# Turning the stored sums of a Strassen-type down-projection: block transposes and transfers through memory in place of TensorE transposes

## The chip, the cores and the metric

One Trainium2 chip; the kernel runs on one core. The metric is the device time of one execution in microseconds (us). Engines in the profile: PE is TensorE (PEld its weight loads), DVE VectorE, ACT ScalarE, POOL GpSimd, SP SyncE.

## The reference, cut to what matters

One layer of a trunk: attention and a short gated convolution side by side, merged by gates, then a squared-ReLU MLP, then a gated per-layer embedding. Sequence 256, width 2048, MLP width 8192, all float32. The change lies in the MLP:

```python
h = rms_norm(r, g_mlp[i])
r = r + jnp.square(jax.nn.relu(h @ w_up[i])) @ w_down[i]
h = rms_norm(r, g_ple[i])
r = r + jax.nn.sigmoid(h @ w_ple_gate[i]) * (p[i] @ w_ple_proj[i])
```

## The kernel before, in words

Float32 matmuls are done in two parts: each operand is split into a high and a low part (`high` on ScalarE, `low` on VectorE), and three products of the parts are added in PSUM.

The MLP is one loop, `for g in range(NU)`, of 72 steps of a little over 8 us each. In step g TensorE runs `cols(...)`, a unit of the up-projection (64 units, tile `ps_up`) or, in the last 8 steps, of a part of the down-projection that is done plainly (`ps_dn`). From step 7 these sums have only one of the eight PSUM banks, bank 7. Beside it in the step `products` runs the rest of the down-projection by seven products P1 to P7 of sums of quarters of the operands (the scheme of Strassen and Winograd), each in a bank of its own. The weights for that are made by VectorE and ScalarE one step ahead (`make`: `b`, `t13`, `t24`, `s`, `s_raw`), and ScalarE copies the unit's sum out of bank 7 within `make` (`take`, `evacuated`: tiles `up`, `dn`). `load` issues weight transfers on SP's queue; the accumulating transfers go on GpSimd's queue, among them `t<-raw_s` (line 704), which adds one weight block to another on its way.

The seven products belong to two halves of the output rows ("sides"). At the end of a group they are stored to memory, `part_...` (`store`), and added up there. For the stored groups, `fetch_part(side, h)` brings the parts back at steps 53, 56, 59 and 62 into four tiles `part_in`, VectorE adds them with scales in ten jobs, three a step (`run_jobs`), and each call ends in two sums of [256 tokens × 256 columns], u = 4·side + h and 4·side + 2 + h, which lie tokens first. The residual `r_kept[u]` in memory lies columns first, so each sum must be turned.

Before, `turn_part` does it on TensorE: four transposes of 128 × 128 into `ps_part`, in bank 7, between two runs of `products`; `out` copies the bank on ScalarE into a tile `part_out`, and GpSimd issues a transfer that adds it to `r_kept[u]` (line 883). `turns_due`, `queue` and `due` fix that one sum is turned in a step. `load_r` (line 958) reads `r_kept` back: u = 4 to 7 at step 64, 0 and 1 at step 68, 2 and 3 at step 69.

All small tiles come from one pool with one tag (`slot`) and rotate: a tile gets the room of the tile that was handed out a full round earlier, and its first writer waits until all that read that one are done, transfers included. GpSimd's queue issues in the order of the code; each of its transfers takes one of 8 semaphores in turn, and so also waits for the transfer 8 places before it.

Of the kernel before, what the change touches and what calls it, by code (L numbers as in the profile page):

```python
# [18 lines left out]
P = 128  # L19
# [19 lines left out]
def hybrid_block_kernel(ctx: ExitStack, tc: tile.TileContext, ins: dict, out: bass.AP):  # L39
# [29 lines left out]
    def bank(name):  # L69
        return psum("acc", [P, CW], name)  # L70
# [665 lines left out]
    def make(a, xs, evacuate, work):  # L736


        w, j = wS[a], a[1]
        raw = w["raw"]  # L740
        flat, halves = "p a f -> p (a f)", "p (a f) -> p a f"
        fresh = None
        if 0 in xs:
            if j not in sums:
                fresh = sum_u(j)
                sums[j] = tuple(slot([P, 4, P], F32R, f"s_{i}") for i in range(2))
            sh, sl = sums[j]
            for i, name in enumerate(("S1", "S3", "S2", "S4")):
                w[name] = sh[:, i, :], sl[:, i, :]
            if a in NATIVE:  # L750
                w["S1"], w["S3"] = fresh[:, 0, :], fresh[:, 1, :]
                fresh, sh, sl = (t[:, 2:, :] for t in (fresh, sh, sl))
            hi, lo = half_tiles("b")
            keep(w, ("B11", "B22"), hi, lo)
            src = raw[:, 0:2, :].rearrange(flat)
            high(hi, src)
            evacuate()
            if fresh is not None:
                high(sh, fresh)
            low(lo, src, hi)  # L760
            if a in ADDED:
                t13 = w["t13"]
            else:
                t13 = raw[:, 0:3:2, :]
                dve.tensor_add(t13, raw[:, 0:2, :], raw[:, 2:3, :].to_broadcast([P, 2, CW]))
            w["raw13"] = t13
        if 2 in xs:
            b21 = w["B21"] = tuple(slot([P, CW], F32R, f"b21_{n}") for n in range(2))
            high(b21[0], raw[:, 3, :])
            evacuate()  # L770
            out_turned()
            fill()
            dve.tensor_add(raw[:, 1, :], raw[:, 1, :], w["raw13"][:, 0, :])
            if 0 in xs:
                low(b21[1], raw[:, 3, :], b21[0])
                dve.tensor_add(raw[:, 3, :], raw[:, 1, :], raw[:, 3, :])
                raw24 = raw[:, 1:4:2, :]
            else:
                dve.tensor_add(raw[:, 2, :], raw[:, 1, :], raw[:, 3, :])
                low(b21[1], raw[:, 3, :], b21[0])  # L780
                raw24 = raw[:, 1:3, :]
                work()
        if 0 in xs:
            if fresh is not None:
                low(sl, fresh, sh)
            if 2 not in xs:
                work()
            out_turned()
            if a in NATIVE:
                w["T1"], w["T3"] = w["raw13"][:, 0, :], w["raw13"][:, 1, :]  # L790
                fill()
            else:
                t13 = half_tiles("t13")
                keep(w, ("T1", "T3"), *t13)
                view = [t.rearrange(halves, a=2) for t in t13]
                high(view[0], w["raw13"])
                fill()
                low(view[1], w["raw13"], view[0])
        if 2 in xs:
            t24 = half_tiles("t24")  # L800
            keep(w, ("T2", "T4"), *t24)
            view = [t.rearrange(halves, a=2) for t in t24]
            high(view[0], raw24)
            fill()
            low(view[1], raw24, view[0])
# [37 lines left out]
    def scaled(dst, src, by, other, how=ALU.add):  # L843
        dve.scalar_tensor_tensor(dst, src, by, other, op0=ALU.mult, op1=how)

    jobs, turns_due = [], []

    def fetch_part(side, h):
        tiles = {}
        for names in (("P2", "P4"), ("P3", "P5"), ("P1", "z"), ("P7", "P6")):  # L850
            t = slot([P, 2, S], F32, "part_in")
            for i, name in enumerate(names):
                tiles[name] = t[:, i, :]
                if name != "z":
                    load(tiles[name], parts[side, name][:, h * S:(h + 1) * S])
        p1, p2, p3, p4, p5, p6, p7, z = (tiles[n] for n in ("P1", "P2", "P3", "P4", "P5", "P6", "P7", "z"))

        def first():
            act(z, p1, AF.Copy, scale=up0)
            act(p1, p1, AF.Copy, scale=up1)  # L860

        jobs.extend((
            first,
            lambda: scaled(p7, p7, up1, p1),
            lambda: scaled(p2, p2, up0, z),
            lambda: scaled(p7, p6, up1, p7),
            lambda: scaled(z, p5, up0, z, ALU.subtract),
            lambda: scaled(p4, p4, up1, p7),
            lambda: (scaled(p3, p3, up0, z), turns_due.append((4 * side + h, (p2, p4)))),
            lambda: scaled(p5, p5, up1, p7, ALU.subtract),  # L870
            lambda: (scaled(p3, p6, down0, p3), turns_due.append((4 * side + 2 + h, (p3, p5)))),
        ))

    def turn_part(u, src):
        ps = bank("ps_part").rearrange("p (i s) -> p i s", i=2)
        for i in range(2):
            for t in range(NT):
                inorder(nc.tensor.transpose(ps[:, i, t * P:(t + 1) * P], src[t][:, i * P:(i + 1) * P], ident))

        def out():  # L880
            st = slot([P, 2, S], F32, "part_out")
            act(st, ps, AF.Copy)
            nc.gpsimd.dma_start(r_kept[u], st, accum_op=ALU.add)

        turned_out.append(out)

    filling, turned_out = [], []

    def out_turned():
        while turned_out:  # L890
            turned_out.pop(0)()

    def fill(n=1):
        for _ in range(min(n, len(filling))):
# [62 lines left out]
        r[u] = slot([P, 2, S], F32, f"r_{u}")  # L957
        nc.gpsimd.dma_start(r[u], r_kept[u])

    fetching = {53: (1, 0), 56: (1, 1), 59: (0, 0), 62: (0, 1)}  # L960

    for g in range(2):
        load_raw(g)
# [6 lines left out]
    for g in range(NU):  # L970
# [10 lines left out]
        for a, x in staged[g + 2]:  # L981
            if x == 0:
                load_added(a)
        if g in fetching:
            fetch_part(*fetching[g])
        for u in {NU - 8: (4, 5, 6, 7), NU - 4: (0, 1), NU - 3: (2, 3)}.get(g, ()):
            load_r(u)
        if g == NU - 3:
# [39 lines left out]
            dn_done(*units[n][1], evac.pop(n))  # L1028
        taken = []

        queue = [] if ending else list(staged[g - 1])

        def take():
            if taken:
                return
            taken.append(evacuated(ps, kind))
            if ending:
                side = staged[g - 1][0][0][0]
                filling.extend(lambda name=name: store(side, name) for name in NAMES)
            if due and queue:  # L1040
                products(*queue.pop(0))
                turn_part(*due.pop(0))

        due = [turns_due.pop(0)] if turns_due and queue else []

        def run_jobs():
            for _ in range(min(3, len(jobs))):
                jobs.pop(0)()

        fill(carried)  # L1050
        if staged[g]:
            make(staged[g][0][0], [x for _, x in staged[g]], take, run_jobs)
        take()
        out_turned()
        if g == NU - 1:
            p1 = [evacuated(prod["P1"], "p1", by) for by in (up0, up1)]
            d, e = (slot([P, CW], F32, n) for n in "de")
# [12 lines left out]
        if kind == "up" and i == 63:  # L1070
            up_sum(i, evac.pop(g))
            up_high(i)
            up_low(i)
        for a, x in queue:
            products(a, x)
        assert not due
    assert not jobs and not turns_due

# [183 lines left out]
```

## Time and the profile before

| what | number |
|---|---|
| median of 3 runs | 1423.03 us (1422.92 to 1423.10) |
| the profiled execution | 1422.78 us, span 1421.0 us |
| TensorE clock granted | full in all slices |
| `ps_part` transposes | 32, from 1196.1 to 1285.8 us |
| `r_kept<-part_out` issues | 8, from 1197.6 to 1290.0 us |
| `r<-r_kept` issues | 8, from 1237.9 to 1302.1 us |

The span is the time from the first to the last instruction of the profiled execution, and all times of the trace are counted from its start. A row of a timeline reads: start, length, engine, line, operation, tile written <- tiles read, and in brackets the idle time of that engine just before it and what ended it.

### The profile page before, as it was taken

Reading aid. Unit: us, or ns where it says so; the run is one execution under the profiler, and the core shown is the slowest. Engines: PE = TensorE matmul, PEld = TensorE weight load, DVE = VectorE, ACT = ScalarE, POOL = GpSimd, SP = SyncE. Lnnn points to the kernel's source line nnn. Section 1 sums busy time; section 2 is a strip of 40 time slices with the busy share of each in tenths; the row PEclk is TensorE's granted clock in tenths of the full one; section 3 lists DMA queues with packets and bytes.
Section 4 is the critical chain, followed back from the end, with each engine's and each line's share of the span. In section 5 each row is a group of like instructions: output and inputs, shape, how many; then the busy total and the mean of one; then the engine's idle time right before and its main releaser. Section 6 shows DMA issues by size and latency. Waiting matters only on the chain.

```text
span 1421.0 us, 19899 instructions
## 1 busy us (share of the span) xinstructions
PE 1410.7 (99%) x7031; PEld 1192.5 (84%) x7031; DVE 1103.0 (78%) x1685; ACT 880.8 (62%) x1441; POOL 209.6 (15%) x319
## 2 busy tenths in 40 slices
PE   9999999999999999999999999999999999999998
PEld 7888888888888888888888888888888888778888
DVE  7666666766455656665999999999999997798984
ACT  7665544554535444446777777777777876666752
POOL 0034464311120200000010101101010100121000
PEclk9999999999999999999999999999999999999999
DMA  9868787765666675663788887989899899999470
GB/s 295 298 216 262 220 243 229 235 224 198 217 202 213 214 259 194 218 210 107 214 291 239 271 243 236 271 256 271 254 239 276 230 297 279 295 266 275 151 257 23
DMA packets 222708, 333.50 MB, mean 235 GB/s; under 512 B 13840, under 2 KB 147216, under 8 KB 208528
## 3 DMA queue, kind: packets, MB, share of 16 engines
q1 hardware_dynamic: 202944, 287.08, 61.9%
q0 software_dynamic: 19520, 45.11, 14.0%
q8 instruction: 55, 0.90, 0.2%
q14 instruction: 45, 0.37, 0.1%
q10 hardware_dynamic: 144, 0.04, 0.0%
HBM read 294.43 MB, written 24.64 MB: 225 GB/s over the span
## 4 chain that ended last, share of the span: by engine, by line
PE 95%; DMA 2%; DVE 1%; issue 1%; ACT 1%; POOL 0%; SPq 0%; DVEq 0%; POOLq 0%; ACTq 0%
PE ps_up L90 24%; PE P L90 18%; PE ps_g L90 12%; PE ps_o L90 7%; PE ps_pg L90 6%; PE ps_y L90 6%; PE ps_q L90 3%; PE ps_k L90 3%; PE ps_cx L90 3%; PE ps_cb L90 3%; PE ps_cc L90 3%; PE ps_v L90 3%; PE ps_dn L90 1%; PE ps_proj L90 1%; DMA t<-raw_s 1%
## 5 line engine op out<-in xcount | busy, mean ns | idle before, releaser
L101 DVE TENSOR_TENSOR w_lo<-raw,w_hi 128x512 fp32r<-128x512 f32 (+1 forms) x524 | 468.0, 926 | 187.1 <-ACT w_hi L87 161.5
L87 ACT ACTIVATE w_hi<-raw 128x512 fp32r<-128x512 f32 (+1 forms) x524 | 406.9, 816 | 258.9 <-PE ps_g L90 62.6
L90 PE MATMUL ps_up<-x,w_hi 128*128 128x512 f32 x1024 | 255.0, 392 | 0.0
L90 PEld LDWEIGHTS ps_up<-x,w_hi 128*128 128x128 f32 x1024 | 192.1, 188 | 39.3 <-issue 1.7
L90 PE MATMUL ps_g<-w_hi,x 128*128 128x512 f32 x512 | 158.1, 389 | 0.0
L87 ACT ACTIVATE t_hi<-raw_s 128x1024 fp32r<-128x1024 f32 x88 | 93.4, 1062 | 85.3 <-DVE raw_s L101 85.0
L90 PEld LDWEIGHTS ps_up<-x,w_lo 128*128 128x128 f32 x1024 | 131.3, 191 | 5.0
L90 PE MATMUL ps_up<-x,w_lo 128*128 128x256 f32 x1024 | 132.8, 283 | 0.0
L90 PE MATMUL P<-t_hi,s 128*128 128x512 f32 x316 | 115.3, 391 | 0.0
L90 PEld LDWEIGHTS ps_g<-w_hi,x 128*128 128x128 f32 x512 | 96.1, 188 | 19.9
L101 DVE TENSOR_TENSOR t_lo<-raw_s,t_hi 128x1024 fp32r<-128x1024 f32 x88 | 106.3, 1220 | 5.6 <-ACT t_hi L87 5.5
L101 DVE TENSOR_TENSOR raw_s<-raw_s 128x512 f32<-128x512 f32 (+1 forms) x120 | 100.1, 834 | 4.1
L90 PE MATMUL ps_g<-w_lo,x 128*128 128x512 f32 x256 | 99.6, 389 | 0.0
L704 POOL DMA_DIRECT2D t<-raw_s x24 | 20.5, 854 | 454.8 <-DMA raw_s<-in_w_down_dram 121.4
L90 PE MATMUL ps_y<-w_hi,x 128*128 128x512 f32 x256 | 79.4, 389 | 0.0
L87 ACT ACTIVATE up<-ps_up 128x512 f32<-128x512 f32 x64 | 37.9, 593 | 57.7 <-PE ps_up L90 54.0
L101 DVE TENSOR_TENSOR b_lo<-raw_s,b_hi 128x1024 fp32r<-128x1024 f32 x56 | 68.2, 1218 | 4.0 <-ACT b_hi L87 3.9
L90 PEld LDWEIGHTS P<-t_hi,s 128*128 128x128 f32 x316 | 59.4, 188 | 12.0
L90 PE MATMUL ps_pg<-x,w_hi 128*128 128x512 f32 (+1 forms) x272 | 67.9, 380 | 0.7 <-DVE x L101 0.7
L90 PE MATMUL P<-t_lo,s 128*128 128x512 f32 x158 | 61.5, 389 | 0.0
L87 ACT ACTIVATE a<-a 128x256 f32<-128x256 f32 x128 | 53.2, 415 | 12.5 <-DVE a L101 10.6
L87 ACT ACTIVATE b_hi<-raw_s 128x1024 fp32r<-128x1024 f32 x56 | 58.8, 1050 | 0.1
(240 smaller groups left out, 2569.5 us busy)
## 6 DMA issues: line engine op xcount, KB each, us to landing
raw<-in_w_up_dram SPq DMA_DIRECT2D x64, 1024.0 KB, 7.5
raw<-in_w_in_dram SPq DMA_DIRECT2D x56, 1024.0 KB, 5.4
raw_s<-in_w_down_dram SPq DMA_DIRECT2D x200, 256.0 KB, 4.5
raw<-in_w_branch_dram SPq DMA_DIRECT2D x16, 1024.0 KB, 5.8
raw<-in_w_o_dram SPq DMA_DIRECT2D x16, 1024.0 KB, 5.0
raw_first<-in_w_qkv_dram SPq DMA_DIRECT2D x48, 256.0 KB, 6.4
raw<-in_w_qkv_dram SPq DMA_DIRECT2D x12, 1024.0 KB, 6.5
t<-in_w_down_dram SPq DMA_DIRECT2D x48, 256.0 KB, 5.4
```

The source lines that it names most:

```text
L87: return inorder(nc.scalar.activation(*args, **kw))
L90: return inorder(nc.tensor.matmul(*args, **kw))
L101: return lambda *args, **kw: inorder(getattr(nc.vector, name)(*args, **kw))
L704: nc.gpsimd.dma_start(wS[a]["t13"], raw[:, 0:2, :], accum_op=ALU.add)
```

## The change

`fetch_part` becomes `add_parts`. The jobs are eleven and run four a step. The last additions of each sum are followed by a job `turn`: VectorE transposes the sum in blocks of 32 × 32 into a pair of `part_in` tiles that are no longer needed (P1 and z for the first, P7 and P6 for the second). One step later `out` writes this to memory (`turned_s`, two transfers of 128 KB), another step later `back` reads it with `turn_in` (four transfers of 64 KB, in pieces of 32 floats) into a new `part_out`, so that the blocks come to their turned places, and one step after that the accumulating transfer into `r_kept[u]` is issued. What is due stands in `later`, by step, and is issued at the start of the step, before `add_parts` and `load_r`. All these transfers are on GpSimd's queue. The pairs of parts are loaded in another order. `turn_part`, its `out`, `out_turned`, `turns_due`, `queue` and `due` are gone: 32 transposes on TensorE, 8 copies on ScalarE and the use of bank 7 for them. New are 8 block transposes, 16 transfers out and 32 back.

```diff
+        for names in (("P1", "z"), ("P7", "P6"), ("P2", "P4"), ("P3", "P5")):
+            t = pairs[names[0]] = slot([P, 2, S], F32, "part_in")
...
+        def turn(u, src, room):
+            flat = "p a s -> p (a s)"
+            dve.transpose(room.rearrange(flat), src.rearrange(flat))
+            rows_out = turned_room(f"turned_s_{u}", columns=S)
+
+            def out():
+                for t in range(NT):
+                    nc.gpsimd.dma_start(rows_out[t * P:(t + 1) * P, :], room[:, t, :])
+
+            def back():
+                st = slot([P, 2, S], F32, "part_out")
+                turn_in(st, rows_out)
+                later.setdefault(step[0] + 1, []).append(lambda: nc.gpsimd.dma_start(r_kept[u], st, accum_op=ALU.add))
+
+            later.setdefault(step[0] + 1, []).append(out)
+            later.setdefault(step[0] + 2, []).append(back)
...
-            lambda: (scaled(p3, p3, up0, z), turns_due.append((4 * side + h, (p2, p4)))),
+            lambda: scaled(p3, p3, up0, z),
+            lambda: turn(4 * side + h, pairs["P2"], pairs["P1"]),
+            lambda: scaled(p3, p6, down0, p3),
             lambda: scaled(p5, p5, up1, p7, ALU.subtract),
-            lambda: (scaled(p3, p6, down0, p3), turns_due.append((4 * side + 2 + h, (p3, p5)))),
+            lambda: turn(4 * side + 2 + h, pairs["P3"], pairs["P7"]),
...
-    def turn_part(u, src):
-        ps = bank("ps_part").rearrange("p (i s) -> p i s", i=2)
-        for i in range(2):
-            for t in range(NT):
-                inorder(nc.tensor.transpose(ps[:, i, t * P:(t + 1) * P], src[t][:, i * P:(i + 1) * P], ident))
-
-        def out():
-            st = slot([P, 2, S], F32, "part_out")
-            act(st, ps, AF.Copy)
-            nc.gpsimd.dma_start(r_kept[u], st, accum_op=ALU.add)
...
+        step[0] = g
+        for work in later.pop(g, ()):
+            work()
+        if g in adding:
+            add_parts(*adding[g])
...
-            if due and queue:
-                products(*queue.pop(0))
-                turn_part(*due.pop(0))
...
-            for _ in range(min(3, len(jobs))):
+            for _ in range(min(4, len(jobs))):
                 jobs.pop(0)()
```

`turn_in` is an older function of the kernel, used for the attention's and the convolution's tiles:

```python
    def turn_in(dst, src):
        blocks = src.rearrange("(a i) (n b j) -> b i n a j", i=32, b=4, j=32)
        for b in range(4):
            nc.gpsimd.dma_start(dst[b * 32:(b + 1) * 32].rearrange("i n (a j) -> i n a j", j=32), blocks[b])
```

On GpSimd's queue, around the accumulate into `r_kept` of u = 7, there stood before (`t13` is the tile that the trace calls `t`; what is in brackets are the semaphores waited for):

```order
L704 DMA t13_11358<-raw_s_11457 128x1024 [waits DMAHW1_49,DMAHW2_49,DMASW5_49,DMAHW3_49,DMASW1_49,DMAHW4_49,DVE_49,PE_49]
L883 DMA r_kept_5_4719<-part_out_11613 128x512 [waits DMASW6_49,Activation_49]
L704 DMA t13_11535<-raw_s_11624 128x1024 [waits DMAHW0_49,DMAHW2_49,DMASW7_49,DMAHW3_49,DMASW2_49,DMAHW7_49,DVE_49,PE_49]
L883 DMA r_kept_7_4721<-part_out_11704 128x512 [waits Activation_49]
L958 DMA r_4_11819<-r_kept_4_4718 128x512 [waits DMASW3_49,PE_49]
```

and now:

```order
L704 DMA t13_11365<-raw_s_11464 128x1024 [waits DMAHW2_49,DMAHW3_49,DMAHW1_49,DMAHW4_49,DMASW3_49,PE_49]
L420 DMA part_out_11551<-turned_s_5_11451 32x16x32 [waits DMASW1_49,DMASW0_49]
L420 DMA part_out_11551<-turned_s_5_11451 32x16x32 x3
L867 DMA turned_s_7_11530<-part_in_11110 128x256 [waits DVE_49]
L867 DMA turned_s_7_11530<-part_in_11110 128x256
L872 DMA r_kept_5_4719<-part_out_11551 128x512 [waits DMASW6_49,DMASW5_49,DMASW7_49,DMASW4_49,DMASW2_49]
L420 DMA part_out_11641<-turned_s_7_11530 32x16x32 [waits DMASW1_49,DMASW0_49,DMASW3_49,DVE_49,Activation_49]
L420 DMA part_out_11641<-turned_s_7_11530 32x16x32
L704 DMA t13_11548<-raw_s_11636 128x1024 [waits DMAHW3_49,DMAHW2_49,DMAHW7_49,DMAHW0_49,PE_49]
L420 DMA part_out_11641<-turned_s_7_11530 32x16x32 x2
L872 DMA r_kept_7_4721<-part_out_11641 128x512 [waits DMASW6_49,DMASW7_49,DMASW4_49,DMASW3_49]
```

Between the accumulates of u = 5 and u = 7 there are now four transfers back, two of them behind the accumulate of `t`, and the transfers out of u = 7 stand ahead of the accumulate of u = 5.

On TensorE, at the end of step 62, there stood before:

```order
L90 MATMUL P3_10775<-b_hi_11593,s_0_11591 128x512
L90 MATMUL P3_10775<-b_lo_11594,s_0_11591 128x512
L90 MATMUL P3_10775<-b_hi_11593,s_1_11592 128x512
L878 MATMUL ps_part_11699<-ident_90,part_in_11110 128x128 x4
L90 MATMUL P5_10779<-t13_11358,s_raw_11586 128x512
L90 MATMUL P7_10783<-t13_11358,s_raw_11586 128x512
L90 MATMUL ps_up_63_11724<-x_4789,w_hi_11675 128x512
```

and now:

```order
L90 MATMUL P3_10775<-b_hi_11613,s_0_11611 128x512
L90 MATMUL P3_10775<-b_lo_11614,s_0_11611 128x512
L90 MATMUL P3_10775<-b_hi_11613,s_1_11612 128x512
L90 MATMUL P5_10779<-t13_11365,s_raw_11606 128x512
L90 MATMUL P7_10783<-t13_11365,s_raw_11606 128x512
L90 MATMUL ps_up_63_11739<-x_4789,w_hi_11693 128x512
```

The four transposes are gone from between the products; the rest of the order is the same. By step, the block transposes stand in 56 (u = 4), 57 (6), 59 (5), 60 (7), 62 (0), 63 (2) and 65 (1 and 3), and the accumulates are issued in 59, 60, 62, 63, 65, 66 and 68 (both).

More of the change, by code (lines that the diff above doesn't have):

```diff
@@ L770, in make @@
             evacuate()
-            out_turned()
             fill()
@@ L787, in make @@
                 work()
-            out_turned()
             if a in NATIVE:
@@ L844, in scaled, with add_parts @@
         dve.scalar_tensor_tensor(dst, src, by, other, op0=ALU.mult, op1=how)
[L846 to L851, printed above, removed]
+    jobs, later = [], {}
+    def add_parts(side, h):
+        tiles, pairs = {}, {}
+        for names in (("P1", "z"), ("P7", "P6"), ("P2", "P4"), ("P3", "P5")):
+            t = pairs[names[0]] = slot([P, 2, S], F32, "part_in")
             for i, name in enumerate(names):
@@ L868, in fetch_part @@
             lambda: scaled(p4, p4, up1, p7),
-            lambda: (scaled(p3, p3, up0, z), turns_due.append((4 * side + h, (p2, p4)))),
+            lambda: scaled(p3, p3, up0, z),
+            lambda: turn(4 * side + h, pairs["P2"], pairs["P1"]),
+            lambda: scaled(p3, p6, down0, p3),
             lambda: scaled(p5, p5, up1, p7, ALU.subtract),
-            lambda: (scaled(p3, p6, down0, p3), turns_due.append((4 * side + 2 + h, (p3, p5)))),
+            lambda: turn(4 * side + 2 + h, pairs["P3"], pairs["P7"]),
         ))
-    def turn_part(u, src):
-        ps = bank("ps_part").rearrange("p (i s) -> p i s", i=2)
-        for i in range(2):
-            for t in range(NT):
-                inorder(nc.tensor.transpose(ps[:, i, t * P:(t + 1) * P], src[t][:, i * P:(i + 1) * P], ident))
-        def out():
-            st = slot([P, 2, S], F32, "part_out")
-            act(st, ps, AF.Copy)
[L883 to L891, printed above, removed]
+    filling, step = [], [0]
     def fill(n=1):
@@ L958, in load_r @@
         nc.gpsimd.dma_start(r[u], r_kept[u])
-    fetching = {53: (1, 0), 56: (1, 1), 59: (0, 0), 62: (0, 1)}
+    adding = {53: (1, 0), 56: (1, 1), 59: (0, 0), 62: (0, 1)}
     for g in range(2):
@@ L983, in hybrid_block_kernel @@
                 load_added(a)
-        if g in fetching:
-            fetch_part(*fetching[g])
+        step[0] = g
[3 more added lines that the diff above has]
+            add_parts(*adding[g])
         for u in {NU - 8: (4, 5, 6, 7), NU - 4: (0, 1), NU - 3: (2, 3)}.get(g, ()):
@@ L1029, in hybrid_block_kernel @@
         taken = []
-        queue = [] if ending else list(staged[g - 1])
         def take():
@@ L1039, in take @@
                 filling.extend(lambda name=name: store(side, name) for name in NAMES)
-            if due and queue:
-                products(*queue.pop(0))
-                turn_part(*due.pop(0))
-        due = [turns_due.pop(0)] if turns_due and queue else []
         def run_jobs():
-            for _ in range(min(3, len(jobs))):
+            for _ in range(min(4, len(jobs))):
                 jobs.pop(0)()
@@ L1053, in hybrid_block_kernel @@
         take()
-        out_turned()
         if g == NU - 1:
@@ L1073, in hybrid_block_kernel @@
             up_low(i)
[L1074 to L1077, printed above, removed]
+        if not ending:
+            for a, x in staged[g - 1]:
+                products(a, x)
+    assert not jobs and not later
     half_of = {(n, h): (NU + n // 2 + (1 - h) * LEAD // 2, n % 2) for n in range(LEAD) for h in range(2)}
```

## The prediction

> **What bounds the kernel now.** I read the page first: its busy times and its chain that ended last.
>
> ```profile
> span 1421.0 us, 19899 instructions
> PE 1410.7 (99%) x7031; PEld 1192.5 (84%) x7031; DVE 1103.0 (78%) x1685; ACT 880.8 (62%) x1441; POOL 209.6 (15%) x319
> PE 95%; DMA 2%; DVE 1%; issue 1%; ACT 1%; POOL 0%; SPq 0%; DVEq 0%; POOLq 0%; ACTq 0%
> ```
>
> TensorE is the bound: busy 99% of the span and 95% of the chain. Work taken off it counts, as long as nothing else then arrives late. Next, the instructions on the tile that goes, and TensorE's waits from 1150 to 1320 us, the part of the run in which the stored sums are turned.
>
> ```profile
> L878 PE MATMUL ps_part<-ident,part_in x32: 270/273/329, 1196.1 to 1285.8; 128*128 128x128 f32 x32
> L87 ACT ACTIVATE part_out<-ps_part x8: 579/597/601, 1196.7 to 1286.1; 128x512 f32<-128x512 f32 x8
> ...
> PE ps_part L878 <- ACT dn L87: 1.8, 2, 1.5
> ...
> PE ps_dn L90 <- ACT part_out L87: 0.6, 1, 0.6
> PE ps_part L878 <- ACT up L87: 0.6, 1, 0.6
> ```
>
> So 32 transposes stand in 90 us of a run of 1421, and TensorE waits three times for bank 7 on their account, since they, the step's own sum and the next step's sum all use that one bank: 1.8 + 0.6 + 0.6 = 3.0 us. The timeline of TensorE shows what one turn of four costs, and the starts of some steps:
>
> ```profile
> 1241.20 3.70 PE L90 MATMUL ps_dn<-x,w_hi 128*128 128x512 f32 x15
> ...
> 1250.74 0.66 PE L878 MATMUL ps_part<-ident,part_in 128*128 128x128 f32 x4 [1.49 <-ACT dn L87]
> 1251.15 0.48 PE L90 MATMUL P<-t_hi,s 128*128 128x512 f32 x1
> ...
> 1252.40 3.57 PE L90 MATMUL ps_dn<-x,w_hi 128*128 128x512 f32 x15
> ...
> 1287.09 3.56 PE L90 MATMUL ps_dn<-x,w_hi 128*128 128x512 f32 x15
> ```
>
> Matmuls overlap, so the price is from one start to the next: 1251.15 − 1250.74 = 0.41 us for four, not 4 × 0.273. Step 64 lasts from 1241.20 to 1252.40 = 11.2 us; the four steps from 1252.40 to 1287.09 take 8.7 on average. Step 64 is where this stretch is weakest.
>
> The windows of the trace say how full the other resources are (columns: length, busy time of PE, PEld, DVE, ACT, POOL, then granted clock, DMA share, GB/s):
>
> ```profile
> 1050.00:1100.00 50.00, 50.00 (x259) 42.95 (x259) 46.85 (x62) 36.65 (x55) 5.26 (x7) 1.00 1.00 266
> ...
> 1198.00:1215.00 17.00, 17.00 (x89) 13.73 (x87) 15.79 (x28) 12.99 (x21) 2.19 (x3) 1.00 1.00 296
> ...
> 1233.00:1252.00 19.00, 17.18 (x89) 13.77 (x88) 15.90 (x26) 12.20 (x20) 2.79 (x5) 1.00 0.77 251
> 1252.00:1270.00 18.00, 17.36 (x94) 14.59 (x93) 17.25 (x28) 11.98 (x17) 3.44 (x4) 1.00 1.06 279
> 1270.00:1287.00 17.00, 16.66 (x93) 14.14 (x92) 12.49 (x21) 9.69 (x13) 3.95 (x5) 1.00 1.02 291
> ...
> 1303.00:1320.00 17.00, 15.28 (x81) 12.22 (x80) 14.86 (x26) 9.48 (x16) 0.00 (x0) 1.00 0.49 167
> ```
>
> The DMA engines are full almost throughout, and the change gives work to them. That they are full is not in itself a loss: from 1050 to 1100 the share is 1.00 and TensorE is busy 50.00 of 50.00 us. What counts is which transfer is waited for.
>
> **The change part by part.**
>
> *Transposes removed.* 8 turns × 0.41 = 3.3 us off TensorE, all of it on the path.
>
> *Waits on bank 7 removed.* 3.0 us as above. The largest, 1.49 us at 1250.74, comes from a late copy of the step's sum; without the transposes the next user of the bank is the following step's first matmul, several products later, so I take the wait as gone. Gain so far: 3.3 + 3.0 = 6.3 us.
>
> *ScalarE's copies removed.* 8 × 0.597 = 4.8 us, on an engine busy 12.20 of 19.00 us at its busiest there: no direct gain.
>
> *Block transposes added to VectorE.* The same operation stands earlier in this kernel, on the same 128 × 512 floats (from the rows of its tile), and transfers out and back of the new kind have rows too (GpSimd's busy time and mean ns of one issue; then KB and median us to landing):
>
> ```profile
> L101 DVE STREAM_TRANSPOSE blocks<-q x4: 665/685/705, 75.5 to 105.6; 128x512 f32<-128x512 f32 x4
> ...
> L420 POOL DMA_DIRECT2D uT<-turned_uT x16 | 10.7, 704 | 5.9 <-issue 3.9 <-DMA qkT<-turned_q 1.8
> ...
> turned_uT<-blocks POOLq DMA_DIRECT2D x4, 256.0 KB, 3.0
> uT<-turned_uT POOLq DMA_DIRECT2D x16, 64.0 KB, 6.2
> turned_cbT<-blocks POOLq DMA_DIRECT2D x4, 256.0 KB, 4.5
> cbT<-turned_cbT POOLq DMA_DIRECT2D x16, 64.0 KB, 3.7
> ```
>
> 8 × 0.685 = 5.5 us. Two of them fall in step 65, where VectorE has 18.00 − 17.25 = 0.75 us free: 2 × 0.685 − 0.75 = 0.6 us late. Elsewhere 17 − 15.79 = 1.2 us (step 59 and 60) or more covers one. Cost 0.6 us (0 if the next step takes it up, 1.4 if not covered at all).
>
> *Four jobs a step in place of three, and the parts loaded in another order.* The same additions run in the same window; I cost them at nothing, with VectorE's free time above as the cover.
>
> *Transfers added.* Each sum is written out (2 × 128 KB), read back (4 × 64 KB) and then accumulated as before: 8 × 512 KB = 4.2 MB. The page has the two kinds of queue:
>
> ```profile
> q1 hardware_dynamic: 202944, 287.08, 61.9%
> q0 software_dynamic: 19520, 45.11, 14.0%
> ```
>
> q0 moved 45.11 MB in 14.0% of 1421 us, 227 GB/s of all engines; q1 326 GB/s. So the new work is 4.2/326 = 12.9 to 4.2/227 = 18.5 us of all 16 engines. The hole in the windows is 0.23 × 19 = 4.4 us, in 1233 to 1252, and 0.51 × 17 = 8.7 us after 1303. The engines therefore run some 8 to 14 us behind until about 1303, and then catch up. Most of what is behind is loaded a step or more ahead. What is not is in these rows: ScalarE's waits from 1165 to 1320 us, GpSimd's timeline, one row of the chain, the timelines of ScalarE and VectorE, and the landings of `part_out`.
>
> ```profile
> ACT t_hi L87 <- DMA t<-raw_s: 5.2, 2, 3.9
> ...
> ACT x L87 <- DMA r_kept<-part_out: 1.4, 1, 1.4
> ...
> 1227.93 0.85 POOL L704 DMA_DIRECT2D t<-raw_s  x1 [3.51 <-DMA part_in<-part_P]
> 1232.74 0.85 POOL L883 DMA_DIRECT2D r_kept<-part_out  x1 [3.96 <-ACT part_out L87]
> ...
> 1232.74 6.48 DMA r_kept<-part_out
> ...
> 1239.30 0.42 ACT L87 ACTIVATE x<-a 128x256 fp32r<-128x256 f32 x1 [1.41 <-DMA r_kept<-part_out]
> ...
> 1240.09 0.28 DVE L101 TENSOR_TENSOR s_raw<-a 128x128 f32<-128x128 f32 x1
> ...
> 1245.53 0.87 ACT L87 ACTIVATE a<-a 128x256 f32<-128x256 f32 x2 [2.81 <-DVE a L101]
> ...
> DMA to landing us min/median/max: 4.2/7.0/11.9
> ```
>
> The accumulates `t<-raw_s` are waited for already, 5.2 us in two places. What the backlog costs TensorE lies between 0 (the stretch from 1050) and the 8 us at which the backlog begins, if all of it reaches such a transfer. I take 2.0, nearer the low end, because that stretch stood as full for 50 us without a stall.
>
> *Waits added.* Each part_out now holds its room (the tiles of this pool rotate) from the turn_in until its accumulate lands, and turn_in, the accumulates of `t` and those into `r_kept` go through GpSimd's one queue in order: a `t` that waits for its loads holds up the turn_ins behind it, and they the sums. The place that decides is u = 7. Before, its accumulate was issued at 1232.74 and landed 6.48 us later (the chain's row); ScalarE's x waited 1.41 us for that room, and VectorE's `s_raw` of step 63 followed at 1240.09. Step 64's x hangs on this: at 1245.53 ScalarE waits 2.81 us for VectorE. Now the room of u = 7 goes to `s_raw` itself, and two of the four turn_ins stand behind the `t` that ran at 1227.93, which its loads set and not TensorE. 1227.93 + 0.85 + 2 × 0.70 = 1230.2; the last turn_in lands 3.7 to 6.2 us after its issue at 1229.5, so by 1234.5 (between the two); the accumulate then takes 7.0, to 1241.5. That is 1.4 us later than `s_raw` ran before. The gain had by then, three turns and one wait, 3 × 0.41 + 0.6 = 1.8 us, is lost with it: cost 1.4 + 1.8 = 3.2 us. Bounds: with the shortest landing, 4.2, `s_raw` could run at 1238.7, about when x leaves it free to (1240.09 − 1.41): 0 to 1.8; with the longest, 11.9, 4.9 more: 8.1. The accumulates of u = 4, 6 and 5 free rooms in steps 59 to 62; by the same working they land within 3 us of the need, on engines with 4 us free per step (12.99 of 17.00 on ScalarE): 0 taken, 3 at most.
>
> *Sum.* −6.3 + 0.6 (VectorE) + 2.0 (DMA) + 3.2 (room of u = 7) = −0.5 us. The profiled execution took 1422.78 us (the span and 1.8 us around it), so it becomes 1422.3; the median of the runs, 1423.03, stands 0.25 higher: 1422.5.
>
> The row and a rule that speaks against the change: four 64 KB transfers back take 3.7 to 6.2 us each to land, as long as or longer than the 256 KB written out in one (3.0 to 4.5). The Trainium skill, "DMA: Bandwidth & Descriptors", section Specifications, says that transfers of under 512 bytes a piece miss the line rate because the engine reads, modifies and writes; here the pieces are 32 floats, 128 bytes. The rows agree in kind. By that rule the DMA term would stand at its upper end, +8 rather than +2, and the sum at +5.5 us.
>
> **The rivals.**
>
> *Clean win.* Everything that was added hides, and all of 6.3 us is had: 1423.03 − 6.3 = 1416.7. Step 64 alone lasts 11.2 us against 8.7, so that up to 2.5 more could go, 1414.2. For it: the full stretch 1050 to 1100 without a stall; against it: rooms are freed by landings, and some of these are waited for before already.
>
> *Room of step 63.* The accumulate of u = 7 lands at its longest, 1246.4; `s_raw` and with it step 64 start 4.9 us later than in the forecast: 1422.5 + 4.9 = 1427.4. It decides as soon as the landing is past 1242: from there each microsecond is one of the whole. For it: the queue in order, and a wait of 1.41 us for the same landing before. Against it: half of the landings took 7.0 or less.
>
> *DMA engines behind.* `t<-raw_s` and the weights of the next units land late by the whole 8 us: the sum becomes +5.5, 1428.5. For it: shares of 1.00 to 1.06 in three of the windows shown. Against it: the full stretch from 1050. The Trainium skill's rule on short pieces, above, is on its side. It decides once the backlog is longer than the lead of the loads.
>
> *The change does not free the bank.* Should the waits on bank 7 move to the next step's first matmul, only 3.3 us are gained: 3.0 worse than forecast, 1425.5. The row at 1250.74 says the bank was free 1.66 us before the next step began, so I give it little.
>
> **How the numbers follow.** The forecast (a gain of about 6 us, nearly all given back in steps 59 to 67) has 0.37, the clean win 0.33, the room of step 63 at its long end 0.15, the DMA engines 0.12, the bank 0.03. A change of under 0.2%, 2.85 us, is about what a measurement of this kernel can't tell from none. The forecast lies within it in 0.30 of its 0.37 (0.04 below, 0.03 above); the clean win is faster in 0.30 of its 0.33; the room and the DMA engines are slower in 0.25 of their 0.27; the bank's case is slower in 0.02. So faster 0.34, same 0.36, slower 0.30. The range goes from 1415.5, between the clean win's two times, to 1428.5, the DMA case; about 0.1 is left out at each side. The forecast's own range is 1419 to 1426.
>
> **What would show it.** No `ps_part` rows, and TensorE's rows from 1190 to 1290 with no wait for `up` or `dn` at line 878's place: the gain. `s_raw` of step 63 with idle time put down to DMA `r_kept<-part_out`: the room. `t_hi` waiting for `t<-raw_s` longer than 5.2 us in all, and landings of `t` and of the weights above 8 us: the DMA engines. Block transposes at 0.69 us with VectorE not idle: the 5.5 us. Step 64 well under 11.2 us, and the clean win holds; longer, and the room did it. The prediction is wrong if a landing differs from its earlier row by several microseconds (all prices of the transfers come from a stage with other neighbours), or if the stretch after 1303 doesn't move with the steps before it.

## The result, and the profile after

The changed kernel takes 1441.03 us (median of 4 runs, 1440.65 to 1442.38) against 1423.07 before: a ratio of 1.0128 (95% interval 1.011 to 1.0145), 18 us slower. The forecast was 1422.5 and its range ended at 1428.5. Times are medians over executions in the fast state; one execution of e11 (2013.72 us at a mean granted clock of 0.65) is left out, and since it is the profiled one, e11 has no trace to compare.

The page of the changed kernel, its first lines and its chain:

```profile
span 1438.9 us, 19932 instructions
PE 1412.9 (98%) x6999; PEld 1193.7 (83%) x6999; DVE 1108.7 (77%) x1693; ACT 876.2 (61%) x1433; POOL 240.7 (17%) x367
PE 94%; DMA 3%; DVE 1%; ACT 1%; issue 0%; POOL 0%; SPq 0%; POOLq 0%; DVEq 0%
```

TensorE has 32 instructions fewer. From 1130 us on it now waits for other things than bank 7:

```profile
PE ps_dn L90 <- ACT x L87: 6.4, 1, 6.4
PE ps_up L90 <- ACT up L87: 5.2, 1, 5.2
PE ps_dn L90 <- ACT dn L87: 4.1, 3, 3.3
PE P L90 <- ACT t_hi L87: 2.4, 1, 2.4
```

These are 18.1 us in six waits, where before there were 3.2 us of this kind. The starts of the steps, read off TensorE's timelines (the first matmul of each step), say where they lie:

| stretch | before | after | difference |
|---|---|---|---|
| steps 58 to 61 | 34.34 | 32.60 | −1.7 |
| step 62 | 9.48 | 13.96 | +4.5 |
| step 63 | 8.23 | 9.88 | +1.6 |
| step 64 | 11.20 | 16.45 | +5.3 |
| steps 65, 66 | 17.32 | 16.38 | −0.9 |
| steps 67 to 69 | 25.21 | 33.19 | +8.0 |
| from step 70 to the end | 126.07 | 127.45 | +1.4 |

Two waits for an accumulate into `r_kept` stand behind steps 62 to 64. From ScalarE's and VectorE's waits (1180 to 1320 us), two rows and one row:

```profile
ACT b L87 <- DMA r_kept<-part_out: 8.4, 1, 8.4
ACT t_hi L87 <- DMA t<-raw_s: 8.0, 1, 8.0
...
DVE s_raw L101 <- DMA r_kept<-part_out: 8.4, 1, 8.4
```

`b` of step 62 got the room of u = 5, `s_raw` of step 63 that of u = 7. GpSimd's timeline shows why these came free late:

```profile
1215.29 0.86 POOL L704 DMA_DIRECT2D t<-raw_s  x1 [0.98 <-DMA raw_s<-in_w_down_dram]
1216.41 2.75 POOL L420 DMA_DIRECT2D part_out<-turned_s  x4 [0.26 <-issue]
1219.07 1.22 POOL L867 DMA_DIRECT2D turned_s<-part_in  x2
1228.42 0.87 POOL L872 DMA_DIRECT2D r_kept<-part_out  x1 [8.13 <-DMA part_out<-turned_s]
1230.50 1.39 POOL L420 DMA_DIRECT2D part_out<-turned_s  x2 [1.21 <-DMA turned_s<-part_in]
1232.05 0.93 POOL L704 DMA_DIRECT2D t<-raw_s  x1 [0.16 <-DMA part_in<-part_P]
1232.65 1.74 POOL L420 DMA_DIRECT2D part_out<-turned_s  x2
1243.05 0.92 POOL L872 DMA_DIRECT2D r_kept<-part_out  x1 [8.65 <-DMA part_out<-turned_s]
```

The accumulate of u = 5 waits 8.13 us at the head of the queue for its transfers back. The transfers back of u = 7 stand behind it, and then wait 1.21 us more for their own transfers out, which were issued at 1219.07 and took 9.9 us to land. The accumulate of u = 7 then waits 8.65 us more. It is issued at 1243.05, before at 1232.74. The landings tell where these waits come from (issues of 1232 to 1234 us, then of 1230.4 to 1232 us; the last number is the median time to landing):

```profile
t<-raw_s POOLq DMA_DIRECT2D x1, 512.0 KB, 9.6
part_out<-turned_s POOLq DMA_DIRECT2D x2, 64.0 KB, 9.3
...
part_out<-turned_s POOLq DMA_DIRECT2D x2, 64.0 KB, 5.3
```

The two transfers back issued ahead of `t` landed in 5.3 us. The two behind it took 9.3 and landed at 1242.06 and 1242.48, just after `t` itself (1241.63). It was the same at 1216.41: `t` landed at 1225.28, the four transfers back behind it at 1226.23 to 1227.87, the two out at 1228.66 and 1229.82. While the compute engines stood, SP could not load, for the tiles to load into were still in use, and the DMA engines ran half empty (40 slices of 1181 to 1319 us; the dip is at about 1250 to 1267), and then everything wanted them at once:

```profile
SPq L96 <- DVE w_lo L101: 19.6, 2, 18.7
...
DMA  9998999999999999999903465999999999989999
...
raw_s<-in_w_down_dram SPq DMA_DIRECT2D x18, 256.0 KB, 10.5
```

That is steps 67 to 69: `t_hi` waits 8.0 us for `t`, whose loads landed late. The three `raw_s` loads issued at 1270 to 1275 us took 15.8 us to land (median), the three of the same place in order before, issued at 1255 to 1265, took 10.3.

The waits are not the whole loss. TensorE's idle time, the span less its busy time, grew by 15.7 us (26.0 against 10.3), and its busy time grew by 2.2 us although 32 transposes are gone. The granted clock shows why. In the windows below it is the third number from the right (the last row is the kernel before). The two rows of TensorE's timeline show the same kind of matmul at each clock:

```profile
1233.28:1240.10 6.82, 4.58 (x11) 3.61 (x12) 5.05 (x8) 4.87 (x8) 1.12 (x2) 0.50 1.02 301
1253.76:1260.58 6.82, 3.43 (x8) 2.68 (x9) 4.92 (x8) 4.73 (x8) 4.34 (x7) 0.50 0.40 117
1301.54:1304.95 3.41, 2.95 (x8) 2.26 (x8) 3.34 (x7) 0.62 (x3) 1.29 (x3) 0.50 0.84 153
1332.27:1335.68 3.41, 3.40 (x11) 2.99 (x12) 2.77 (x6) 1.97 (x3) 0.00 (x0) 0.50 0.00 0
...
1227.11 0.40 PE L90 MATMUL P<-b_hi,x 128*128 128x512 f32 x1
1258.20 0.63 PE L90 MATMUL P<-b_hi,x 128*128 128x512 f32 x1
...
1050.00:1420.00 370.00, 361.99 (x1950) 307.94 (x1949) 312.43 (x480) 236.34 (x365) 35.29 (x44) 1.00 0.80 236
```

In these four stretches TensorE ran at half its clock and was busy for 14.36 us. Half of that, 7.2 us, is my estimate of what the clock cost: 2.3 in step 63, 1.7 in step 64, 1.5 around step 69 and 1.7 behind step 70. So some 7 of the 18 us are not waits but matmuls that ran slower. The first two stretches begin 2.9 and 3.0 us after TensorE ran dry (at 1230.4 and 1250.8). The four profiles without such a stretch (before, e3, e6 and e18) have no idle time of TensorE over 1.7 us at once in the MLP. How long a stall it takes is not shown: after the 3.3 us from 1286.4 the clock stayed full until 1301.5. That the stalls bring the low clock on is read from these traces; no run tests it. The same estimate gives 4.2 us in e2, 4.7 in e16, 1.6 in e1 and 1.4 in e7.

### The profile page after: what moved, and what is told of

Same layout as the page of the kernel before. It is cut to its first block, busy times and chain, and to the rows that moved or that the text cites. A ratio compares the mean times of both kernels' runs of the same rounds, so it can differ in the third digit from the quotient of the medians.

```text
span 1438.9 us, 19932 instructions
## 1 busy us (share of the span) xinstructions
PE 1412.9 (98%) x6999; PEld 1193.7 (83%) x6999; DVE 1108.7 (77%) x1693; ACT 876.2 (61%) x1433; POOL 240.7 (17%) x367
## 4 chain that ended last, share of the span: by engine, by line
PE 94%; DMA 3%; DVE 1%; ACT 1%; issue 0%; POOL 0%; SPq 0%; POOLq 0%; DVEq 0%
PE ps_up L90 24%; PE P L90 17%; PE ps_g L90 12%; PE ps_o L90 7%; PE ps_pg L90 6%; PE ps_y L90 6%; PE ps_k L90 3%; PE ps_q L90 3%; PE ps_cx L90 3%; PE ps_cb L90 3%; PE ps_cc L90 3%; PE ps_v L90 3%; PE ps_dn L90 1%; DMA raw_s<-in_w_down_dram 1%; DMA part_out<-turned_s 1%; PE ps_proj L90 1%
```

## The experiments

The two theories: (1) rooms (the places in on-chip memory that tiles take in turn): tiles are held by transfers that GpSimd's queue issues in order, and engines wait for these tiles; the late loads follow. (2) bytes: the DMA engines are full, and 4.2 MB more make all transfers late.

**e1: no transposes at all**, the prize by itself.

```diff
-        ps = bank("ps_part").rearrange("p (i s) -> p i s", i=2)
-        for i in range(2):
-            for t in range(NT):
-                inorder(nc.tensor.transpose(ps[:, i, t * P:(t + 1) * P], src[t][:, i * P:(i + 1) * P], ident))
...
-            act(st, ps, AF.Copy)
+            for i in range(2):
+                act(st[:, i, :], src[i], AF.Copy)
```

> The kernel before, with the 32 transposes on TensorE left out: ScalarE copies each sum unturned from its part_in tiles to part_out (the result therefore adds unturned sums), bank 7 is not touched by it, and the accumulate is issued as before. This prices what could be won at most. Forecast's first two terms: 3.3 us of transposes and 3.0 us of waits on bank 7 go, 1416.8 us. Rival: the waits move to the next step's first matmul, and only 3.3 us go, 1419.8 us.

1422.53 us, ratio 0.9992 (0.9983 to 1.0002): neither expectation. At the start of step 63 TensorE was 3.5 us ahead (1229.48 against 1232.97), at that of step 64 only 0.8, for ScalarE waited for the accumulates of u = 5 and u = 7. That of u = 7 was issued 1.7 us sooner than before (1231.00 against 1232.74) and took 7.4 us to land:

```profile
1228.84 0.60 ACT L87 ACTIVATE up<-ps_up 128x512 f32<-128x512 f32 x1 [3.48 <-DMA r_kept<-part_out]
...
1238.49 0.42 ACT L87 ACTIVATE x<-a 128x256 fp32r<-128x256 f32 x1 [3.50 <-DMA r_kept<-part_out]
```

Then the clock was half from 1240.2 to 1243.6 us. So even free turning would have won next to nothing in this kernel.

**e2: rooms for part_out.** (Three more edits, not shown, pay for it: eight temporaries in place of ten, and two small tiles put among them.)

```diff
-                st = slot([P, 2, S], F32, "part_out")
+                st = bp.tile([P, 2, S], F32, tag="part_out", name="part_out", bufs=2)
```

> The changed kernel, with two rooms of their own for the part_out tiles (paid for by two of ten small temporary tiles and two small tiles moved into those), so that no other tile waits for an accumulate to land. Theory 1 (rooms: the 8.4 us waits of ScalarE in step 62 and of VectorE in step 63, and all late loads in steps 66 to 69 follow from them): the waits vanish and the loss with them, 1417 to 1420 us. Theory 2 (DMA engines: the added transfers make the loads and t late by themselves): the stalls of steps 62 to 64, some 14 us, go, those of steps 66 to 69, some 9 us, stay: 1427 us or more.

1429.75 us, ratio 1.0043 (1.0027 to 1.0059): 11 us of the loss go, some 6 stay, between the two expectations. Steps 62 to 64 take 32.5 us (40.3 in the changed kernel, 28.9 before), steps 67 to 69 29.3 (33.2 and 25.2). What stays is partly rooms again, now of the `part_in` pairs that are being written out, and partly late loads and `t` in steps 66 to 68, and the clock (from ScalarE's timeline):

```profile
1229.31 0.42 ACT L87 ACTIVATE x<-a 128x256 fp32r<-128x256 f32 x1 [4.97 <-DMA turned_s<-part_in]
...
1243.30 0.63 ACT L87 ACTIVATE s<-s_raw 128x512 fp32r<-128x512 f32 x1 [5.02 <-DMA turned_s<-part_in]
...
1268.49 1.06 ACT L87 ACTIVATE t_hi<-t 128x1024 fp32r<-128x1024 f32 x1 [4.71 <-DMA t<-in_w_down_dram]
...
1288.59 1.06 ACT L87 ACTIVATE t_hi<-t 128x1024 fp32r<-128x1024 f32 x1 [6.36 <-DMA t<-raw_s]
```

**e3: the bytes alone**, added to the kernel before (with eight temporaries in place of ten, to make room).

```diff
+        def ghost(rows_out=rows_out):
+            for t in range(NT):
+                nc.gpsimd.dma_start(rows_out[t * P:(t + 1) * P, :], row0[0])
+        ghosts.setdefault(at + 1, []).append(ghost)
+        ghosts.setdefault(at + 2, []).append(lambda rows_out=rows_out: turn_in(ghost_in, rows_out))
```

> The kernel before, with the same 16 transfers out and 32 back added on GpSimd's queue at the same steps, from and to tiles that nobody else waits for (the data is not used; the transposes on TensorE stay). Theory 1: TensorE hardly notices, 1423 to 1426 us. Theory 2: t and the weights land late, 1430 us or more.

1422.77 us, ratio 0.9994 (0.9984 to 1.0003). But it answers another question: nothing tied the transfers to their steps, and they were issued from 648 to 704 us. There the 4.2 MB cost nothing that shows.

**e4: long pieces.**

```diff
-                turn_in(st, rows_out)
+                rows = rows_out.rearrange("(n p) s -> p n s", n=2)
+                for b in range(4):
+                    nc.gpsimd.dma_start(st[b * 32:(b + 1) * 32], rows[b * 32:(b + 1) * 32])
```

> The changed kernel, with the four transfers back reading pieces of 1 KB in the stored order in place of pieces of 128 bytes in the turned order (the sums therefore arrive as blocks, not turned). If short pieces make the transfers back land late (median 7.2 us): they land in 4 us or less, the rooms come free some 4 us sooner twice, 1428 to 1433 us. If it is what stands ahead of them in the queue and the full engines: landings stay near 7 us, 1437 to 1442 us.

1443.28 us, ratio 1.0134 (1.0118 to 1.015). The landings of the transfers back, after and here (the 7.2 of the expectation is for these and the accumulates together):

```profile
part_out<-turned_s POOLq DMA_DIRECT2D x32, 64.0 KB, 7.7
```

```profile
part_out<-turned_s POOLq DMA_DIRECT2D x32, 64.0 KB, 6.0
```

A little sooner, and no gain: a wait of VectorE's `b` for an accumulate was 15.1 us here. The short pieces are not what costs. The Trainium skill's rule on pieces under 512 bytes ("DMA: Bandwidth & Descriptors", section Specifications), which the prediction weighed, agrees in kind with these landings, 1.7 us sooner, and it does not decide the time.

**e5: the bytes, tied to their steps.** As e3, with the activation of a recent unit as the source, and one column of the result used:

```diff
+            src = u_raw[max(u_raw)]
...
+            ghosts.setdefault(at + 4, []).append(lambda u=u: dve.tensor_scalar_mul(ghost_sum[:, u:u + 1], ghost_in[:, 0, :1], 0.0))
```

> The kernel before, with 16 transfers out and 32 back added that now stand in steps 57 to 67 (e3's were issued from 648 to 704 us, since nothing tied them to the steps): each writes the activation of a recent unit out, reads it back in the turned order into one spare tile, and of it one column times zero is used. Nobody else waits for them; the transposes on TensorE stay. Theory 1 (rooms, nothing else): 1423 to 1425 us. Theory 2 (the added transfers make the other transfers of the stretch late): landings of part_out and t a few us longer, step 64 and steps 66 to 68 longer, 1428 us or more.

1443.81 us, ratio 1.0146 (1.0126 to 1.0166), as slow as the change itself. It does not tell the theories apart, though, for its waits are not those that it was to be free of: the accumulate of u = 4 stood behind the ghosts in GpSimd's queue and held ScalarE's `s` in step 59, and the probe itself held VectorE (ScalarE's and VectorE's timelines):

```profile
1210.92 0.42 ACT L87 ACTIVATE s<-s_raw 128x256 fp32r<-128x256 f32 x1 [5.98 <-DMA r_kept<-part_out]
...
1281.12 0.15 DVE L101 TENSOR_SCALAR ghost_sum<-ghost_in 128x1 f32<-128x1 f32 x1 [5.16 <-DMA ghost_in<-turned_s]
```

What it shows: the transfers are enough for a room wait, with the transposes still on TensorE and no sum turned by them.

**e6 and e7: rooms for part_out in the kernel before, and in e1.** The same line as in e2.

> The kernel before, with two rooms of their own for part_out (paid for as in e2). If the wait of ScalarE's x in step 63 for the accumulate of u = 7 (1.41 us, and 3.5 us where the transposes were left out) is what makes step 64 long: step 64 falls from 11.2 by 1.4 us or more, 1420.5 to 1422 us. If step 64 is long for other reasons: unchanged, 1423 us.

1421.03 us, ratio 0.9988 (0.9979 to 0.9998); step 64 fell from 11.20 to 9.54 us. The room of u = 7 did cost the kernel before 1.7 us there.

> e1 (no transposes on TensorE, sums added unturned) with two rooms of their own for part_out. e1 was 3.5 us ahead at the start of step 64 and lost it again there and at step 66. If the rooms took it back: 1417 to 1419 us. If loads and t that come no sooner took it back (the DMA engines as the second bound): 1421 to 1422.5 us.

1419.81 us, ratio 0.9976 (0.9966 to 0.9985): between the two. (The lead of 3.5 us in the expectation stood at the start of step 63, not 64.) At the start of step 68 it was 6.8 us ahead of the kernel before (1271.21 against 1278.03), about the 6.3 of the forecast; at the end 3.1 (spans of 1417.9 and 1421.0). The rest went in step 68 (10.50 against 9.06) and after step 70, where the clock was half from 1311.0 to 1314.4.

**e8: transfers out and back on SP's queue.**

```diff
-                    nc.gpsimd.dma_start(rows_out[t * P:(t + 1) * P, :], room[:, t, :])
+                    nc.sync.dma_start(rows_out[t * P:(t + 1) * P, :], room[:, t, :])
...
+                    nc.sync.dma_start(st[b * 32:(b + 1) * 32].rearrange("i n (a j) -> i n a j", j=32), blocks[b])
```

> The changed kernel, with the transfers out and back issued on SP's queue (where the weight loads are) in place of GpSimd's, so that they no longer stand behind t and the accumulates. If standing behind these made the transfers late: they land in 4 to 6 us, the accumulates of u = 5 and 7 come some 5 us sooner each, 1426 to 1432 us. If the full engines make them late: landings stay at 7 us or more, 1437 us or more.

1445.91 us, ratio 1.0164 (1.0146 to 1.0183). The transfers back landed in 5.3 us (median) in place of 7.7, but now the weights stood behind them: TensorE waited 8.8 us for `t<-raw_s` and ScalarE for weight units and, 6.55 us, for `part_out<-turned_s`.

**e9 to e12: a step earlier; with rooms; on ScalarE's queue; one room for all.**

```diff
-            later.setdefault(step[0] + 1, []).append(out)
-            later.setdefault(step[0] + 2, []).append(back)
+            out()
+            later.setdefault(step[0] + 1, []).append(back)
```

> The changed kernel, with every transfer issued a step earlier: the transfers out in the step of the block transpose, the transfers back one step later, the accumulate one step after that. If the steps put between the transfers are what keeps the rooms too long: the waits in steps 62 and 63 (8.4 us each) fall to 2 us or less, 1424 to 1430 us. If the transfers themselves are slow because of what else is in flight: the waits only move to other tiles, 1436 us or more.

1434.01 us, ratio 1.0071 (1.0056 to 1.0086). Half of the first expectation: the wait for u = 7 is gone, that for u = 5 stays (7.99 us), and `t_hi` in step 66 waits 9.35 us for `t`.

> e9 with two rooms of their own for part_out as in e2. e2 still had ScalarE's x in step 62 and s in step 63 wait 5.0 us each for the rooms of part_in pairs that were being written out. Theory 1 (rooms of any kind): a step earlier these are free in time, 1419 to 1424 us. Theory 2 (full engines make weights and t late): steps 66 to 69 still lose 5 us or more, 1426 us or more.

1440.36 us, ratio 1.0116 (1.01 to 1.0133): worse than e9 and than e2 alone. ScalarE's `s` of step 63 waits 13.09 us for `turned_s<-part_in`.

> e2 with the transfers out and back on ScalarE's queue in place of GpSimd's, so that they stand behind neither t, nor the accumulates, nor the weight loads. If the order in GpSimd's queue makes them late: they land in 3 to 5 us in place of 6.4 and no part_in pair is waited for, 1420 to 1425 us. If the engines are full: 6 us and more to land, 1428 us or more. ScalarE's own waits for a landing before it issues would show as idle time on ScalarE.

1450.80 us (median of 3, 1448.67 to 1454.75), ratio 1.0193 (1.017 to 1.0217), the slowest. Which wait does it stays open; that this kernel gains nothing by ScalarE's queue is all that it shows.

> The changed kernel with the transfers a step earlier, and for u = 4 to 7 one tile of two rooms of their own that holds the blocks, goes out, is filled again by the transfer back and accumulated, so that no part_in pair and no part_out is waited for by another tile until step 62. Theory 1 (rooms): 1417 to 1421 us. Theory 2 (full engines): 1426 us or more.

1439.11 us, ratio 1.0106 (1.0089 to 1.0123). I had left out the pairs of u = 0 and 2, which are written out as in the change. ScalarE's copy out of bank 7 got the room of one, and that transfer out stood in GpSimd's queue behind the accumulate of u = 7 (ScalarE's, then GpSimd's timeline):

```profile
1250.88 0.60 ACT L87 ACTIVATE up<-ps_up 128x512 f32<-128x512 f32 x1 [15.57 <-DMA turned_s<-part_in]
```

```profile
1232.49 1.36 POOL L704 DMA_DIRECT2D t<-raw_s  x1
1240.37 0.86 POOL L874 DMA_DIRECT2D r_kept<-part_out  x1 [6.51 <-DMA part_out<-turned_s]
1240.94 1.40 POOL L869 DMA_DIRECT2D turned_s<-part_in  x2
```

A block transpose done in step 62 was written out from 1240.94 on and landed at about 1250.9.

**e13 and e14: as many bytes fewer elsewhere**, after and before.

```diff
+                if g in LIGHT:
+                    load(wU[g][0][:, :HALF], w[:, :HALF])
```

> The changed kernel, with eight weight units (59 to 66) loaded by half, 512 KB in place of 1 MB, 4.2 MB fewer in all, as many as the change adds; both halves of the unit's sum use the same half of the weights, with the same matmuls (the result is of other weights). Theory 2 (full engines are the root: everything lands late because the bytes no longer fit): the landings fall and the loss goes, 1417 to 1424 us. Theory 1 (rooms held through three landings in GpSimd's queue, whatever the load): the waits in steps 62 and 63 stay, 1432 us or more.

1436.97 us, ratio 1.0086 (1.0069 to 1.0103): theory 1's number. The two waits are still there, 6.1 and 9.4 us, and the tile part_out's transfers, back and accumulate, still land in 7.5 (7.2 in the changed kernel):

```profile
1231.99 0.63 ACT L87 ACTIVATE b<-raw_s 128x512 fp32r<-128x512 f32 x1 [6.13 <-DMA r_kept<-part_out]
...
1248.77 0.29 DVE L101 TENSOR_TENSOR s_raw<-a 128x128 f32<-128x128 f32 x1 [9.44 <-DMA r_kept<-part_out]
...
DMA to landing us min/median/max: 2.2/7.5/12.1
```

> The kernel before with the same eight units loaded by half: the base for e13. If the loads bound nothing before: 1422 to 1423 us. If the engines were the second bound already: 1418 to 1420 us.

1427.86 us, ratio 1.0029 (1.0019 to 1.0039): slower with fewer bytes, which neither theory had. With the loads moved, `t` was issued ahead of the accumulate of u = 5 and held it, and ScalarE's `up` waited 6.17 us for that room (GpSimd's, then ScalarE's timeline):

```profile
1224.90 0.85 POOL L711 DMA_DIRECT2D t<-raw_s  x1 [12.41 <-DMA part_in<-part_P]
1225.44 1.19 POOL L890 DMA_DIRECT2D r_kept<-part_out  x1
```

```profile
1233.19 0.60 ACT L87 ACTIVATE up<-ps_up 128x512 f32<-128x512 f32 x1 [6.17 <-DMA r_kept<-part_out]
```

**e15 and e16: half the sums each.**

```diff
+        if side in (1,):
+            jobs.extend((
+                first,
...
+                lambda: turn(4 * side + 2 + h, pairs["P3"], pairs["P7"]),
+            ))
+            return
```

In e16 it is `(0,)`; the left-out rows are the jobs of the change.

> Only the sums u = 4 to 7 (those at steps 56 to 63) turned by VectorE and transfers, four jobs a step; u = 0 to 3 by TensorE as before. Theory 1 (rooms are scarce until step 64, plentiful after): nearly the whole loss, 1434 us or more. Theory 2 (bytes): about half of it, 1429 to 1433 us.

1434.72 us, ratio 1.008 (1.006 to 1.01): the four early sums carry 11 of the 18 us. Steps 62 and 63 last 14.16 and 18.15 us, with waits of 9.01 and 7.83 us for `r_kept<-part_out`.

> Only u = 0 to 3 (at steps 62 to 68) by VectorE and transfers; u = 4 to 7 by TensorE as before, with two rooms of their own for their part_out as in e6. Theory 1: little loss, 1420 to 1424 us. Theory 2: about half the loss, 1428 us or more.

1428.58 us, ratio 1.0032 (1.0023 to 1.0042), some 6 to 7.6 us over e6, its base (by the ratios and by the medians): theory 1's range missed. (With three jobs a step the sums u = 1 and 3 arrive after the residual has been read back and are missing from the result.) There is no room wait in its steps 62 to 66; it is 4.6 us ahead of the kernel before at the start of step 66. It loses in steps 66 to 69, where `t_hi` waits 6.99 us for `t<-raw_s`, and after step 70, where `d` waits 1.71 us for the last transfers back. The clock, half for 10.2 us here and never in e6, is by the estimate above 4.7 us of the loss:

```profile
1283.40 1.06 ACT L87 ACTIVATE t_hi<-t 128x1024 fp32r<-128x1024 f32 x1 [6.99 <-DMA t<-raw_s]
```

Why `t` was late there can be read off. It was issued at 1274.09, in e6 at 1270.41. GpSimd had stood idle for 6.72 us, so `t` was itself at the head of the queue, waiting. The three `raw_s` loads issued at 1255 to 1265 us took 14.0 us to land (median), in e6 10.9, and `t` was issued 0.7 and 0.5 us after the second of them had landed.

**e17: e2 and e13 together.**

> The changed kernel with both: two rooms of its own for part_out (e2) and eight weight units loaded by half (e13; the result is of other weights). e2 alone took 11 us off the loss, e13 alone 4 us. If what e2 left, 6 us of it in steps 66 to 69, comes from bytes that no longer fit: 1419 to 1424 us. If it comes from the order in GpSimd's queue: 1427 us or more.

1434.28 us, ratio 1.0081 (1.0067 to 1.0095), slower than e2 although it loads fewer bytes. In e2 the transfer out of u = 0 was issued at 1233.82, ahead of the accumulate of u = 7; here it came behind it, at 1241.00, and ScalarE's `s` waited 10.04 us for the pair (5.02 in e2).

**e18: e6 again.**

> e6 once more, the kernel before with two rooms of their own for part_out, in more rounds: 1421 us, 0.1 to 0.2% faster than before, if the room of u = 7 cost what e6 showed; within 0.1% of before, if e6 was chance.

1420.94 us (11 runs), ratio 0.9989 (0.998 to 0.9998). As e6 had shown, 0.1% faster than the kernel before; step 64 takes 9.55 us.

## Why the prediction was wrong, point by point

*The gain, −6.3.* Mis-sized. Where it arises it is there (6.8 us in e7 at step 68), but the end of the kernel sees 3.1 of it with rooms of their own (e7) and hardly 1 without (e1). I had shown the wait of 1.41 us for the room of u = 7 and still counted the whole gain: what comes next after TensorE is a landing that TensorE does not set.

*The room of u = 7, +3.2, and those of u = 4, 6 and 5, 0.* The step that failed. Right were the place (`s_raw` of step 63), the mechanism (the turn_ins behind `t`, the accumulate behind them) and that it would cost. Wrong were the sizes. I had the last transfer back land by 1234.5, it landed at 1242.48: `t` ran at 1232.05 and not at 1227.93, and the landing took some 9 us and not 3.7 to 6.2, prices from a stage with other neighbours. `t` itself stood behind the accumulate of u = 5 and the first transfers back of u = 7, which ran until 1231.89; its last load, `part_in<-part_P`, also came 4.1 us later than before (issued at 1225.69 against 1221.64). And u = 5, for which I took 0, cost as much: 8.4 us of ScalarE. The kernel before waited for that room already, and longer than for that of u = 7 (ScalarE's waits before, 1180 to 1320 us; the first row is u = 5, in step 62):

```profile
ACT up L87 <- DMA r_kept<-part_out: 3.6, 1, 3.6
ACT x L87 <- DMA r_kept<-part_out: 1.4, 1, 1.4
```

The sum counts the second row and passes over the first. Together with the half clock behind each stall they make +11.4 us in steps 62 to 64. With rooms of its own for part_out (e2) 7.8 us of this go, and 3.9 of steps 67 to 69. I priced each sum's transfers by themselves and `t` at 0.85 us of issue, where transfers behind `t` landed only after it and the next transfer of the chain waits for them.

*A term that was missing: the clock, taken as full.* The prediction says that each microsecond past 1242 is one of the whole. Each cost more: TensorE came out of the stalls at half its clock, an estimated 7.2 us in all, and the sum has no term for it.

*The DMA engines, +2.0 of 0 to 8.* Steps 67 to 69 lost 8.0 us, the upper end; some 1.5 of it is the clock. The mechanism, loads of `t` that land late, was right (15.8 us against 10.3). Its source was in part another: the engines stood half empty behind the stall and then had it all to load. 4.2 MB fewer bytes elsewhere gave only 4 us back (e13), and two kernels with fewer bytes were slower than their bases (e14, e17). The late half of the change by itself loses too, where nothing stalled before (e16). There the trace speaks for full engines, since the loads landed some 3 us later with GpSimd's queue idle; no run takes the one without the other.

*VectorE, +0.6.* 8 transposes took 0.71 us each, 5.7 us in all, and no wait of another engine is put down to them. *Four jobs a step, the other loading order:* no wait shows them, and no run takes either alone. *ScalarE's copies, 0:* the busiest window shown was 12.99 of 17.00 us, not 12.20 of 19.00; nothing hung on it.

*The rivals.* "Room of step 63" had the mechanism and 1427.4 us; it needed a second room, the landings behind `t` and the clock. "DMA engines behind" had 1428.5 and the late loads, but not the stall ahead of them. Both ended where the range ended, since each was priced with the other at its middle value.

*One thing told of the code ahead of the prediction may be loose:* that rooms are handed out after a full round. In these kernels the room of a late accumulate was among the next wanted (`up` and `x` before and in e1, `b` and `s_raw` after), as if rooms were handed out in the order in which they come free. That is an inference; no run shows it.

## What to carry to other kernels

Before pricing a transfer that replaces work on an engine, follow the tile: who gets its room next, and what has to land, in which order of which queue, before it is free. A chain of three transfers in one in-order queue costs three landings of that stretch (some 7 us each here, 9 to 10 behind a 512 KB accumulate), and what holds its head holds all behind it. Price the prize first, too: the same kernel without the replaced work at all (e1) would have shown that there was 1 us to win and not 6. And a stall can cost more than its length: look at the granted clock behind it, since here some 7 us of 18 were lost there.

## What the runs showed of the hardware that I had not expected

A 64 KB transfer landed in 3.7 to 6.2 us (medians) earlier in the kernel, in 7.7 beside the weight loads, in 9.3 to 9.8 when issued right behind the 512 KB `t`, and in 2.3 while the engines stood half empty (1254.87 to 1257.11); pieces eight times as long brought 1.7 of the 7.7. After TensorE had run dry for 5.2 and 6.4 us its granted clock was 0.50 for 6.8 us each, from about 3 us into the stall. And 4.2 MB in 48 more transfers from 648 to 704 us cost nothing that shows (e3).
